# A new order for the first weight loads and adaLN pieces of a conditioned short-convolution layer on one core

## The chip, the core and the metric

The kernel runs on one NeuronCore of a Trainium2 chip. The metric is device time of one execution in microseconds (us); lower is better. TensorE (PE) multiplies and loads weights (PEld), VectorE (DVE) and ScalarE (ACT) do elementwise work, GpSimd (POOL) hardly takes part, and SyncE (SP) issues the loads, one after the other, to 16 DMA engines.

## What is computed

One layer (DEPTH is 1), in float32, for 256 positions, 2048 features and an inner width E of 4096:

```python
h = rmsnorm(x, norm_g)
mod = silu(c) @ ada_w + ada_b            # ada_w: 2048 x 6144
shift, scale, gate = split(mod, 3)
h = h * (1 + scale) + shift
b, c, v, g = split(h @ w_in, 4)          # w_in: 2048 x 16384
u = causal_depthwise_conv(c * v, conv_w) # width 3
y = (b * u * silu(g)) @ w_out            # w_out: 4096 x 2048
out = rmsnorm(x + gate * y, final_g)
```

## The kernel before

Every weight is used once, so the kernel streams 224 MB from HBM. A float32 product is made of three float32r products: ScalarE rounds a loaded tile to `hi` (line 347), VectorE makes `lo`, the rest (line 348), the activations `hT` are split in the same way, and TensorE adds up hi·hi, hi·lo and lo·hi (line 485). So 1 MiB of weights is 48 matmuls, one cast on ScalarE and one subtraction on VectorE.

adaLN must be done before features can be used. `shift` and `scale` are sums over 2048 rows of `ada_w`, weighted by `silu(c)`. The 2048 features are 16 tiles of 128 (numbered from 0) and are made ready two at a time. Tiles 0 and 1 come first, in the opening part of the program (lines 216 to 412). For each later pair VectorE adds up 16 products: 8 **pieces** of 0.5 MiB each, two DMAs and two products to a piece (`ada_piece`, `ada_sums`, lines 434 to 457; the first product of a pair is line 455, the others 457). After the eighth, TensorE transposes the sums, ScalarE adds them up, and `modulate` (line 322) makes the two tiles of `hT`: the high part on ScalarE (339), the rest on VectorE (340 and 341). I number the pieces of tiles 2 and 3 from 0 to 7; 8 and on belong to tiles 4 and 5.

While few tiles are ready, the kernel works on many outputs at once. `plan` (line 56) lists steps: which chunks of 512 outputs of which quarter of `w_in`, with which feature tiles. `parts` (line 523) runs a step in **loads** (`raw_s`) of 1 MiB. I number them: load 1, of 0.5 MiB, is the second step's; loads 2 to 8 take feature tiles 0 and 1 for two chunks each; load 9, used by **block 9** of products, is the first that takes tiles 2 and 3; load 10 and on go back to the first chunks with them. A load's products go to one or two PSUM banks (`mm_s`, three buffers), which ScalarE copies to `acc` (line 517) or VectorE adds (519) before the bank is used again; in a later step ScalarE may first copy `acc` into the bank (533).

What sets the order: the instructions of each engine, and SP's DMAs, run in the order of the built program, each waiting for its inputs and buffers. Within the program a scheduler chooses the order by its own estimates; the kernel ties it down in places. `PACE` says how many adaLN pieces follow each of the first ten loads (the first entry is the opening block, which needs no load here). `first_loads` counts the DMAs that keep the written order on SP, `first_pieces` the loads whose casts and subtractions, with the adaLN products between them, keep it on ScalarE and VectorE. Pieces have four buffers (`at`), loads three (`raw`).

Later the kernel goes through the other outputs with all features ready (`mm_b`, from about 370 us), with the products for `gate` between (`at_g`, lines 616 to 633, already from about 210 us), and at the end through `w_out` (`mm_o`).

Of the kernel before, what the change touches and what calls it, by code (L numbers as in the profile page):

```python
# [49 lines left out]


SHARE = 1.5
PACE = (0, 0, 0, 2, 1, 2, 2, 2, 2, 2)


def plan():
# [36 lines left out]
    while new or any(k < KT for k in done.values()):  # L93
# [30 lines left out]
        if p in order:  # L124
            done[p] = hi
    blocks = [b for step in steps for b in step[-1]][: len(PACE)]
    some = [piece for b in blocks for piece in b]
    for b, n in zip(blocks, PACE):
        b[:], some = some[:n], some[n:]
# [5 lines left out]
def short_conv_layer(ctx: ExitStack, tc: tile.TileContext, x, c, norm_g, ada_w, ada_b, w_in, conv_w, w_out, final_g, out):  # L135
# [83 lines left out]
    for n in range(KT // 4):  # L219
        at = wpool.tile([P, SLOT], F32, tag=("lo", "hi")[n % 2], name="at0", bufs=3)  # L220
        at = at.rearrange("p (k s f) -> p k s f", k=4, s=2)
        if n == 0:
            wpool.tile([P, 32], F32, tag="line3", name="line3", bufs=1)
        for j, kk in ((0, 2), (2, 2)) if n < 3 else ((0, 1), (1, 1), (2, 1), (3, 1)):
            for s in range(2):
                nc.sync.dma_start(at[:, j : j + kk, s, :], adas[:, 4 * n + j : 4 * n + j + kk, s, 0 : NK0 * P])
        first_ada.extend(at[:, i] for i in range(4))
# [239 lines left out]
        modulate(k0, nk, (gs[:, 0:nk], gs[:, nk : 2 * nk]))  # L467

    opener = [None]
    first_loads = [None] * 28  # L470

    def load(dst, src):

# [44 lines left out]
        else:  # L518
            nc.vector.tensor_tensor(out=acc[ch, q], in0=bank, in1=acc[ch, q], op=ALU.add)

    first_pieces = [None] * 10

    def parts(chs, q, k0, k1, seeds, between):

# [272 lines left out]
```

## Time and profile before

| | |
|---|---|
| time, median of 3 runs | 929.32 us (929.06 to 929.54) |
| the profiled execution | 930.7 us, span 928.6 us |
| TensorE busy | 901.8 us (97%) |
| VectorE busy | 629.7 us (68%) |
| ScalarE busy | 453.4 us (49%) |
| mean granted TensorE clock | 0.993 |
| read from HBM | 224.49 MB |

A row of a timeline has start and duration in us, engine, source line, instruction, what it writes and reads with shapes, how many are merged, and in brackets how long the engine was idle before it and what ended that. A matmul's duration is longer than its share of a stream, because matmuls overlap. The span runs from the first to the last instruction; the time of a run includes what lies around it.

### The profile page before, as it was taken

The numbers are of one execution on the slowest core, as the hardware profiler recorded it, in microseconds if no ns is written. First come the engines' busy times: TensorE is split into PE (matmuls) and PEld (weight loads), VectorE is DVE, ScalarE is ACT, GpSimd is POOL, SyncE is SP. The second block draws the span as 40 slices with busy tenths as digits, with TensorE's granted clock in tenths as the row PEclk, the third lists the DMA queues.
The fourth block names the chain that finished last, engine by engine and source line by source line (L and its number), as shares of the span: only waits on it lengthen the run. The fifth ranks groups of instructions, "written<-read, shape, count | busy, mean of one in ns | idle before, by whom it ended". The sixth has DMA issues, their size and how long they took to land.

```text
span 928.6 us, 16211 instructions
## 1 busy us (share of the span) xinstructions
PE 901.8 (97%) x7041; PEld 862.6 (93%) x7041; DVE 629.7 (68%) x603; ACT 453.4 (49%) x431; POOL 2.3 (0%) x9
## 2 busy tenths in 40 slices
PE   7988999999999999999999999999999999999996
PEld 4887999999999989999999999999999988888885
DVE  5678998999897899885455545544554544545882
ACT  6656885565544765643443344334433433344333
POOL 1000000000000000000000000000000000000000
PEclk9998999999999999999999999999999999999999
DMA  9899999999897769667666566656665496556542
GB/s 295 312 315 382 341 360 356 336 341 340 316 342 266 254 245 325 203 214 222 188 200 202 181 192 204 196 183 197 204 188 183 139 359 227 181 191 207 192 136 91
DMA packets 146807, 227.64 MB, mean 245 GB/s; under 512 B 5488, under 2 KB 103840, under 8 KB 146352
## 3 DMA queue, kind: packets, MB, share of 16 engines
q1 hardware_dynamic: 146608, 226.51, 72.6%
q8 instruction: 55, 0.90, 0.4%
q14 instruction: 16, 0.13, 0.0%
q0 software_dynamic: 96, 0.08, 0.0%
q10 hardware_dynamic: 32, 0.01, 0.0%
HBM read 224.49 MB, written 2.10 MB: 244 GB/s over the span
## 4 chain that ended last, share of the span: by engine, by line
PE 83%; DMA 8%; DVE 5%; issue 2%; ACT 2%; SPq 1%; ACTq 0%; DVEq 0%
PE mm_b L485 37%; PE mm_s L485 26%; PE mm_o L693 6%; PE mm_o L694 6%; PE mm_o L695 6%; DMA at<-in_ada_w_dram 3%; DMA raw_s<-in_sc_w_in_dram 3%; DMA at_g<-in_ada_w_dram 2%; DVE lo L348 2%; ACT hi L347 1%; DVE gacc L625 1%; DVE gv L457 1%; DVE acc L419 0%; DVE acc L422 0%; PE tp_g L464 0%
## 5 line engine op out<-in xcount | busy, mean ns | idle before, releaser
L485 PE MATMUL mm_s<-hT,hi 128*128 128x256 f32 x2048 | 342.1, 279 | 13.1 <-ACT acc L517 4.2
L485 PE MATMUL mm_b<-hT,hi 128*128 128x256 f32 x2048 | 348.4, 276 | 0.0
L485 PEld LDWEIGHTS mm_s<-hT,hi 128*128 128x128 f32 x2048 | 303.0, 190 | 15.8 <-ACT acc L517 4.8
L485 PEld LDWEIGHTS mm_b<-hT,hi 128*128 128x128 f32 x2048 | 308.2, 188 | 0.0
L485 PE MATMUL mm_b<-hT,lo 128*128 128x256 f32 x1024 | 282.6, 276 | 0.0
L485 PE MATMUL mm_s<-hT,lo 128*128 128x256 f32 x1024 | 263.4, 277 | 0.0
L348 DVE TENSOR_TENSOR lo<-raw,hi 128x2048 fp32r<-128x2048 f32 x64 | 146.7, 2292 | 133.6 <-ACT hi L347 133.6
L347 ACT CAST hi<-raw 128x2048 fp32r<-128x2048 f32 x64 | 122.4, 1913 | 199.9 <-PE mm_b L485 152.4
L485 PEld LDWEIGHTS mm_b<-hT,lo 128*128 128x128 f32 x1024 | 192.2, 188 | 0.1
L485 PEld LDWEIGHTS mm_s<-hT,lo 128*128 128x128 f32 x1024 | 184.1, 189 | 0.0
L347 ACT CAST hi<-raw_s 128x2048 fp32r<-128x2048 f32 (+1 forms) x64 | 121.5, 1899 | 109.8 <-PE mm_s L485 84.4
L348 DVE TENSOR_TENSOR lo<-raw_s,hi 128x2048 fp32r<-128x2048 f32 (+1 forms) x64 | 145.4, 2272 | 28.9 <-ACT hi L347 26.4
L348 DVE TENSOR_TENSOR lo<-raw_o,hi 128x2048 fp32r<-128x2048 f32 x32 | 73.3, 2291 | 64.3 <-ACT hi L347 64.3
L347 ACT CAST hi<-raw_o 128x2048 fp32r<-128x2048 f32 x32 | 61.0, 1907 | 106.8 <-PE mm_o L695 85.3
L694 PE MATMUL mm_o<-lo,y 128*128 128x512 f32 x256 | 99.3, 389 | 0.0
L695 PE MATMUL mm_o<-hi,y 128*128 128x512 f32 x256 | 99.3, 389 | 0.0
L693 PE MATMUL mm_o<-hi,y 128*128 128x512 f32 x256 | 99.3, 389 | 0.0
L457 DVE SCALAR_TENSOR_TENSOR gv<-at,silu_c,gv 128x512 f32<-128x512 f32 x105 | 78.5, 749 | 2.3 <-DMA at<-in_ada_w_dram 0.6
L695 PEld LDWEIGHTS mm_o<-hi,y 128*128 128x128 f32 x256 | 48.1, 188 | 10.0
L693 PEld LDWEIGHTS mm_o<-hi,y 128*128 128x128 f32 x256 | 48.1, 188 | 9.9
L694 PEld LDWEIGHTS mm_o<-lo,y 128*128 128x128 f32 x256 | 48.1, 188 | 9.9
L517 ACT COPY acc<-mm_s 128x1024 f32<-128x1024 f32 x43 | 42.9, 1013 | 16.8 <-PE mm_s L485 16.8
(109 smaller groups left out, 376.5 us busy)
## 6 DMA issues: line engine op xcount, KB each, us to landing
raw<-in_sc_w_in_dram SPq DMA_DIRECT2D x64, 1024.0 KB, 5.6
raw_s<-in_sc_w_in_dram SPq DMA_DIRECT2D x63, 1024.0 KB, 7.1
raw_o<-in_sc_w_out_dram SPq DMA_DIRECT2D x32, 1024.0 KB, 5.2
at<-in_ada_w_dram SPq DMA_DIRECT2D x124, 256.0 KB, 7.2
at_g<-in_ada_w_dram SPq DMA_DIRECT2D x32, 512.0 KB, 6.7
x<-in_x_dram SPq DMA_DIRECT2D x4, 512.0 KB, 6.5
big<-in_x_dram SPq DMA_DIRECT2D x2, 1024.0 KB, 7.3
out_dram<-big SPq DMA_DIRECT2D x4, 512.0 KB, 2.9
```

The source lines that it names most:

```text
L347: nc.scalar.copy(hi[:, :n], raw[:, :n])
L348: nc.vector.tensor_tensor(out=lo[:, :n], in0=raw[:, :n], in1=hi[:, :n].bitcast(F32), op=ALU.subtract)
L457: nc.vector.scalar_tensor_tensor(out=gv, in0=at4[:, i], scalar=c_k, in1=gv, op0=ALU.mult, op1=ALU.add)
L485: mm = last_mm[0] = nc.tensor.matmul(dst, w, h[:, k], start=begins and left, stop=ends, skip_group_check=True)
L517: nc.scalar.copy(acc[ch, q], bank)
L625: nc.vector.scalar_tensor_tensor(out=ga, in0=at3[:, i, :], scalar=s, in1=ga, op0=ALU.mult, op1=ALU.add)
L693: nc.tensor.matmul(po, yh, hi[:, o], start=opens, stop=False, skip_group_check=True)
L694: nc.tensor.matmul(po, yh, lo[:, o], start=False, stop=False, skip_group_check=True)
L695: nc.tensor.matmul(po, yl, hi[:, o], start=False, stop=ct == NCT - 1, skip_group_check=True)
```

## The change

Four numbers change, and no arithmetic.

```diff
-PACE = (0, 0, 0, 2, 1, 2, 2, 2, 2, 2)
+PACE = (0, 0, 2, 1, 2, 1, 2, 1, 2, 2)
...
-        for j, kk in ((0, 2), (2, 2)) if n < 3 else ((0, 1), (1, 1), (2, 1), (3, 1)):
+        for j, kk in ((0, 2), (2, 2)) if n < 3 else ((0, 2), (2, 1), (3, 1)):
...
-    first_loads = [None] * 28
+    first_loads = [None] * 10
...
-    first_pieces = [None] * 10
+    first_pieces = [None] * 4
```

The pieces that follow the first ten loads are 13 as before, but begin one load sooner and are spread more evenly. Of the opening's adaLN rows for tiles 0 and 1 (`at0`), the last four k rows come as one pair and two single ones, not as four single ones. The order is written out for the first 10 DMAs and for four loads' parts; beyond that the scheduler chooses.

SP, from load 2 on (`raw_s` is a load, `at` a piece, two DMAs each). Before:

```order
L474 DMA raw_s<-in_sc_w_in_dram 128x2x1024 x2
L474 DMA at<-in_ada_w_dram 128x2x256 x4
L474 DMA raw_s<-in_sc_w_in_dram 128x2x1024
L474 DMA at<-in_ada_w_dram 128x2x256 x2
L474 DMA raw_s<-in_sc_w_in_dram 128x2x1024
L474 DMA at<-in_ada_w_dram 128x2x256 x4
L474 DMA raw_s<-in_sc_w_in_dram 128x2x1024
L474 DMA at<-in_ada_w_dram 128x2x256 x4
L474 DMA raw_s<-in_sc_w_in_dram 128x2x1024
L474 DMA at<-in_ada_w_dram 128x2x256 x4
```

and now:

```order
L474 DMA raw_s<-in_sc_w_in_dram 128x2x1024
L474 DMA at<-in_ada_w_dram 128x2x256 x4
L474 DMA raw_s<-in_sc_w_in_dram 128x2x1024
L474 DMA at<-in_ada_w_dram 128x2x256 x4
L474 DMA raw_s<-in_sc_w_in_dram 128x2x1024 x2
L474 DMA at<-in_ada_w_dram 128x2x256 x2
L474 DMA raw_s<-in_sc_w_in_dram 128x2x1024 x2
L474 DMA at<-in_ada_w_dram 128x2x256 x2
L474 DMA raw_s<-in_sc_w_in_dram 128x2x1024
L474 DMA at<-in_ada_w_dram 128x2x256 x2
L474 DMA raw_s<-in_sc_w_in_dram 128x2x1024
L474 DMA at<-in_ada_w_dram 128x2x256 x4
```

Pieces 0 and 1 moved ahead of load 3, pieces 2 and 3 ahead of load 4, piece 4 behind load 5; piece 7 (the first two DMAs of the last row of both) moved from behind load 7 to behind load 9.

VectorE, from load 2's low part on in both (128x2048 is a load's low part, `gv` an adaLN product of tiles 2 and 3). Before:

```order
L348 TENSOR_TENSOR lo<-raw_s,hi 128x2048 x2
L455 TENSOR_SCALAR gv<-at,silu_c 128x512
L348 TENSOR_TENSOR lo<-raw_s,hi 128x2048
L457 SCALAR_TENSOR_TENSOR gv<-at,silu_c,gv 128x512 x3
L348 TENSOR_TENSOR lo<-raw_s,hi 128x2048
L457 SCALAR_TENSOR_TENSOR gv<-at,silu_c,gv 128x512 x5
```

and now:

```order
L348 TENSOR_TENSOR lo<-raw_s,hi 128x2048
L455 TENSOR_SCALAR gv<-at,silu_c 128x512
L457 SCALAR_TENSOR_TENSOR gv<-at,silu_c,gv 128x512
L348 TENSOR_TENSOR lo<-raw_s,hi 128x2048
L457 SCALAR_TENSOR_TENSOR gv<-at,silu_c,gv 128x512
L348 TENSOR_TENSOR lo<-raw_s,hi 128x2048
L457 SCALAR_TENSOR_TENSOR gv<-at,silu_c,gv 128x512
L348 TENSOR_TENSOR lo<-raw_s,hi 128x2048
L457 SCALAR_TENSOR_TENSOR gv<-at,silu_c,gv 128x512 x3
L348 TENSOR_TENSOR lo<-raw_s,hi 128x2048
L457 SCALAR_TENSOR_TENSOR gv<-at,silu_c,gv 128x512 x4
```

Both products of piece 0 now stand ahead of load 3's low part, where before the second stood behind load 4's. From load 4's low part to the low part of `hT` for tiles 2 and 3 (line 341) there stand seven low parts of loads in both programs, with 23 products of line 457 before and 20 now.

ScalarE, from load 4's cast (`hi`) on; the copies are those of the banks of loads 2, 3 and (the last row of the second fence) of the second bank of load 3. Before:

```order
L347 CAST hi<-raw_s 128x2048
L517 COPY acc_401<-mm_s 128x1024
L517 COPY acc_403<-mm_s 128x1024
L347 CAST hi<-raw_s 128x2048
L517 COPY acc_472<-mm_s 128x1024
L517 COPY acc_474<-mm_s 128x1024
L347 CAST hi<-raw_s 128x2048
```

and now:

```order
L347 CAST hi<-raw_s 128x2048
L517 COPY acc_410<-mm_s 128x1024
L347 CAST hi<-raw_s 128x2048
L517 COPY acc_412<-mm_s 128x1024
L517 COPY acc_475<-mm_s 128x1024
L347 CAST hi<-raw_s 128x2048
L517 COPY acc_477<-mm_s 128x1024
```

The second copy of each load moved behind the cast of one more load: that of load 2's second bank from ahead of load 5's cast to behind it.

## The prediction

> **What bounds the kernel now.** I read the page first, then TensorE's timeline for its idle times, then the timelines of the engines named there, each for the same stretch.
>
> ```profile
> span 928.6 us, 16211 instructions
> PE 901.8 (97%) x7041; PEld 862.6 (93%) x7041; DVE 629.7 (68%) x603; ACT 453.4 (49%) x431; POOL 2.3 (0%) x9
> PEclk9998999999999999999999999999999999999999
> ```
>
> TensorE is busy for 97% of the span, so little can be won except where it waits, and the clock row shows one dip, in the fourth slice of 23.2 us. These are its waits once the products have begun (start, duration, instruction, idle time before it and what ended that):
>
> ```profile
> 28.83 2.55 PE L485 MATMUL mm_s<-hT,hi 128*128 128x256 f32 x20 [0.72 <-ACT hi L347]
> 42.05 2.10 PE L485 MATMUL mm_s<-hT,hi 128*128 128x256 f32 x16 [1.22 <-ACT acc L517]
> 56.19 2.10 PE L485 MATMUL mm_s<-hT,hi 128*128 128x256 f32 x16 [2.98 <-ACT acc L517]
> 77.83 0.62 PE L485 MATMUL mm_s<-hT,hi 128*128 128x256 f32 x3 [1.48 <-ACT hT L339]
> 81.29 4.00 PE L485 MATMUL mm_s<-hT,hi 128*128 128x256 f32 x17 [2.84 <-DVE hT L341]
> 104.80 0.50 PE L485 MATMUL mm_s<-hT,hi 128*128 128x256 f32 x2 [1.52 <-ACT mm_s L533]
> 330.99 0.51 PE L485 MATMUL mm_s<-hT,hi 128*128 128x256 f32 x2 [2.19 <-DVE acc L519]
> ```
>
> The two largest together, 1.48 + 2.84 = 4.32 us, come before block 9, the first that needs feature tiles 2 and 3: TensorE ran out of work at 76.35 (77.83 - 1.48) and the tiles were whole only at 81.3. They cost more than their length, as the clock says (columns after the times: busy us and count of PE, PEld, DVE, ACT, POOL, then clock, DMA share, GB/s):
>
> ```profile
> 40.00:45.00 5.00, 3.78 (x33) 3.58 (x32) 3.81 (x4) 4.70 (x4) 0.00 (x0) 1.00 0.52 183
> 45.00:50.00 5.00, 5.00 (x47) 5.00 (x46) 4.93 (x5) 1.95 (x3) 0.00 (x0) 1.00 0.90 247
> 55.00:60.00 5.00, 3.81 (x33) 3.81 (x34) 4.64 (x5) 3.05 (x4) 0.00 (x0) 1.00 0.79 286
> 70.00:75.00 5.00, 5.00 (x46) 5.00 (x46) 5.00 (x9) 4.36 (x12) 0.00 (x0) 1.00 1.05 380
> 75.00:80.00 5.00, 1.97 (x15) 1.57 (x14) 4.41 (x6) 3.27 (x4) 0.00 (x0) 0.90 1.04 393
> 80.00:85.00 5.00, 3.71 (x17) 3.71 (x18) 4.74 (x7) 1.91 (x1) 0.00 (x0) 0.50 1.08 377
> 85.00:90.00 5.00, 5.00 (x42) 5.00 (x41) 2.76 (x4) 2.15 (x2) 0.00 (x0) 0.91 1.06 371
> ```
>
> Work done at a lower clock: 0.10 x 1.97 + 0.50 x 3.71 + 0.09 x 5.00 = 2.5 us lost. So **block 9's late features cost 4.3 + 2.5 = 6.8 us**. Why they are late stands on VectorE, which makes the last part of them (L341):
>
> ```profile
> 41.12 2.29 DVE L348 TENSOR_TENSOR lo<-raw_s,hi 128x2048 fp32r<-128x2048 f32 x1 [2.84 <-ACT hi L347]
> 43.33 2.32 DVE L457 SCALAR_TENSOR_TENSOR gv<-at,silu_c,gv 128x512 f32<-128x512 f32 x3
> 45.57 2.28 DVE L348 TENSOR_TENSOR lo<-raw_s,hi 128x2048 fp32r<-128x2048 f32 x1
> 55.26 2.29 DVE L348 TENSOR_TENSOR lo<-raw_s,hi 128x2048 fp32r<-128x2048 f32 x1 [3.59 <-ACT hi L347]
> 67.98 2.29 DVE L348 TENSOR_TENSOR lo<-raw_s,hi 128x2048 fp32r<-128x2048 f32 x1 [2.03 <-ACT hi L347]
> 80.82 0.75 DVE L341 TENSOR_TENSOR hT<-xs,hT 128x256 fp32r<-128x256 f32 x2
> L457 DVE SCALAR_TENSOR_TENSOR gv<-at,silu_c,gv 128x512 f32<-128x512 f32 x105 | 78.5, 749 | 2.3 <-DMA at<-in_ada_w_dram 0.6
> ```
>
> From load 4's low part (41.12) to the features' end (81.57) are 40.45 us, of which VectorE waited 3.59 + 2.03 = 5.62, both times for ScalarE's cast of a load: 34.8 us are work. The loads were late because SP stood still:
>
> ```profile
> 35.09 9.90 SPq L474 DMA_DIRECT2D at<-in_ada_w_dram  x4
> 45.09 0.41 SPq L474 DMA_DIRECT2D raw_s<-in_sc_w_in_dram  x1
> 51.06 9.31 SPq L474 DMA_DIRECT2D at<-in_ada_w_dram  x4
> 60.46 0.93 SPq L474 DMA_DIRECT2D raw_s<-in_sc_w_in_dram  x2
> ```
>
> For 9.90 us it held the issue of pieces 3 and 4, then for 9.31 us that of pieces 7 and 8, since a piece needs one of four buffers. Piece 4 needs piece 0's, and piece 0's second product stands on VectorE behind load 4's low part, at 43.33. Behind piece 4 stood load 6 (45.09). The DMA engines fell to 183 and 247 GB/s against 380 when fed.
>
> **The change part by part.** It adds and removes no arithmetic. The loads of the first features in fewer pieces save two issues on SP; load 1 is then issued some 0.7 us sooner. That is worth between 0.7 us (the whole wait at 28.83) and nothing, if the DMA engines are the limit there; a loss would need a product to wait for the pair that now lands together, and another two k rows follow it anyway. I take 0.
>
> The rest is one thing, a new order, and I walk it with the durations above. ScalarE's casts give the rate of the stream (each of these casts waited for its own DMA):
>
> ```profile
> 30.41 1.91 ACT L347 CAST hi<-raw_s 128x2048 fp32r<-128x2048 f32 x1 [1.63 <-DMA raw_s<-in_sc_w_in_dram]
> 33.65 1.92 ACT L347 CAST hi<-raw_s 128x2048 fp32r<-128x2048 f32 x1 [0.42 <-DMA raw_s<-in_sc_w_in_dram]
> 39.18 1.91 ACT L347 CAST hi<-raw_s 128x2048 fp32r<-128x2048 f32 x1 [2.71 <-DMA raw_s<-in_sc_w_in_dram]
> 40.99 1.92 ACT L517 COPY acc<-mm_s 128x1024 f32<-128x1024 f32 x2
> 43.21 1.92 ACT L347 CAST hi<-raw_s 128x2048 fp32r<-128x2048 f32 x1 [0.30 <-DMA raw_s<-in_sc_w_in_dram]
> 53.33 1.90 ACT L347 CAST hi<-raw_s 128x2048 fp32r<-128x2048 f32 x1 [6.38 <-DMA raw_s<-in_sc_w_in_dram]
> ```
>
> Loads 2 to 5 came at 30.41, 33.65, 39.18 and 43.21: 12.8 us for 4.5 MiB (a load is 1 MiB, a piece 0.5), 2.84 us per MiB; the steps by themselves give 2.69 to 3.24. In the new order pieces 0 and 1 go ahead of load 3 and pieces 2 and 3 ahead of load 4, so load 3 lands at 30.4 + 2 x 2.84 = 36.1 (2.4 later than now) and load 4 at 41.8 (2.6 later). Then load 5 at 44.6, load 6, behind piece 4, at 48.9 (53.3 now), load 7 at 51.7, load 8 at 56.0, load 9 at 60.2, load 10 at 65.9. No issue holds SP long: both products of piece 0 now stand ahead of load 3's low part, so piece 4's buffer is free by 40.
>
> TensorE pays at first. Load 3's bank waits for the copy of load 1's, which stands behind load 3's cast: 36.1 + 1.8 + 1.0 = 38.9, a wait of 1.0 (TensorE is free at 37.9). Its second bank waits for the copy behind load 4's cast, 41.8 + 1.8 + 1.0 = 44.6, against 41.6: 3.0. Load 4's first bank waits for a copy that now stands behind load 5's cast (ScalarE goes on 44.6 + 1.8 + 1.0 = 47.4, TensorE is free at 47.3): 0.1. After that each copy is done before it is asked for. With the 0.72 at 28.83 that is 4.8, against 0.72 + 1.22 + 2.98 = 4.92 now: TensorE reaches block 9 at 76.2.
>
> VectorE: load 4's low part starts at 41.8 + 1.9 = 43.7. From there to the features the order holds the same seven low parts and 20 adaLN products instead of 23: 34.8 - 3 x 0.75 = 32.6 us, and none of it waits: by the same walk the casts of loads 5 to 10 are over 0.3 to 4 us before VectorE reaches them. The features are whole at 43.7 + 32.6 = 76.3, 5.3 us sooner than now. Block 9's wait falls to 0.1 and the clock has no reason to drop.
>
> Sum: 6.8 (block 9) + 0.1 (waits ahead of it) - 0.1 (what is left) = **6.8 us less** by 105 us. What is late next is the 1.52 us at 104.80 (ScalarE's order, unmoved). Later on only 330.99 shows a wait, so the gain stays. The profiled execution took 930.7 around its span of 928.6, 1.4 above the median of 929.32; taken off the median the time is **922.5 us**.
>
> Bounds: at 3.24 us per MiB load 4 comes at 43.4 and the features at 77.9, 1.6 us worse; at 2.69, 0.6 better for VectorE, but TensorE is then the later one. The wait at 330.99 is hidden or not by VectorE's order among the gate's products, which is new too: between 2.2 us less and (rival 3) all of the gain. I take it as unchanged, since the copy that ends it has the same neighbours.
>
> **The rivals.** 1. The clock drops at the new wait of 3.0 us. At 56.19 a wait of 2.98 left the clock at 1.00, and one pair of 4.32 took it to 0.50, so the point lies between. A drop would cost what it cost in 80 to 85, some 1.9 us: 924.4. The Trainium skill ("TensorE: Matmul & The Clock Gate", Part 1, The HAM clock gate) puts it at an idle window of about 3.4 us that runs freely; both waits of this trace agree, and by that rule this rival needs load 4 to come 0.4 us later than I have it.
>
> 2. One of loads 4 to 6 comes some 2.5 us late, as load 6 did for lack of a full queue. These three have least to spare (0 to 0.5 us), so the features are 2.5 late: 925.0; with the clock dropping again, 927. For it: load 7's issue must wait for load 4's buffer (its low part ends at 45.9), when only load 6 is under way. Against: two loads and a piece are queued ahead until then.
>
> 3. The gain is given back at 330.99. The chain runs from 268 to 331 over VectorE and the gate's DMAs alone:
>
> ```profile
> 246.21 21.83 PE mm_s L485 x192
> 273.67 7.15 DMA at_g<-in_ada_w_dram
> 330.99 67.24 PE mm_s L485 x576
> ```
>
> If it went by its own pace, an earlier TensorE would only wait longer: 929.3. Against it: at its upper end it hangs on TensorE, and 2.19 us in 63 is a small lag.
>
> 4. **Slower.** Piece 7, the last that features 2 and 3 need, is moved on SP from behind load 7 to behind load 9: 11 MiB after load 2 instead of 9, or 2 x 2.84 = 5.7 us later. If SP stands still as it does now, the features come at 81.6 + 5.7 = 87.3 and the time is 935. By the stream piece 7 lands at 30.4 + 11 x 2.84 = 61.6, and VectorE asks for it at about 64; slower than before it is only if SP loses a further 2.4 + 5.3 = 7.7 us, most of a 9.90. VectorE's order around it has room, and piece buffers are freed a load earlier, which speaks against.
>
> **How the numbers follow.** No change is anything within 0.2% (1.9 us, about what a measurement of this kernel can tell). My forecast has 0.49; with the wait at 330.99 gone as well (920.3) 0.06; rival 1 0.13; rival 2 0.14: faster 0.82. Rival 3 or a mixture that nets nothing 0.10. Rival 4 0.08. The range from 919.8 to 928.0 leaves out rival 4 and most of rival 3.
>
> **What would show it.** Right: SP issues loads 4 to 9 with no piece holding it near 10 us; DMA at 350 GB/s or more from 40 to 60; a TensorE wait of about 1 us near 39 and 3 near 44; none over 1 us between 50 and 90, with the clock at 1.00 in 80 to 85; features 2 and 3 whole near 76. Wrong: VectorE waiting for a cast after 46; waits at block 9; a wait near 320 to 335 of more than 3 us, which would mean that the gain was lent, not won.

## The result and the profile after

| kernel | median us | runs | ratio to before (95% interval) |
|---|---|---|---|
| before | 929.19 | 6, 927.70 to 931.46 | 1 |
| changed | 921.45 | 6, 919.56 to 922.25 | 0.9914 (0.9898 to 0.9929) |

The change is worth 7.7 us of 929. The profiled execution of the changed kernel took 920.8 us around a span of 919.0.

The page of the changed kernel: the span, the busy times, and the granted clock in slices of 23 us, which has lost the dip in its fourth slice.

```profile
span 919.0 us, 16211 instructions
PE 898.6 (98%) x7041; PEld 859.8 (94%) x7041; DVE 629.6 (69%) x603; ACT 453.9 (49%) x431; POOL 2.3 (0%) x9
PEclk9999999999999999999999999999999999999999
```

TensorE's timeline of the changed kernel, its waits since the products began (last column: idle time before, and what ended it):

```profile
37.23 2.15 PE L485 MATMUL mm_s<-hT,hi 128*128 128x256 f32 x16 [0.68 <-ACT acc L517]
42.78 3.48 PE L485 MATMUL mm_s<-hT,hi 128*128 128x256 f32 x16 [2.46 <-ACT acc L517]
96.52 0.51 PE L485 MATMUL mm_s<-hT,hi 128*128 128x256 f32 x2 [1.53 <-ACT mm_s L533]
322.91 0.50 PE L485 MATMUL mm_s<-hT,hi 128*128 128x256 f32 x2 [2.40 <-DVE acc L519]
```

No row stands between 43 and 96: block 9 waits for nothing. The two waits at 104.80 and 330.99 are there as before, 8.3 and 8.1 us sooner. Two waits for the copy of a bank are new in place: the prediction had them near 39 and near 44, and they end at 37.23 and 42.78. The second has a drop of the clock behind it. The windows of the changed kernel show that drop, and that there is none in 75 to 85 (columns as in the prediction: clock, DMA share and GB/s last):

```profile
40.00:45.00 5.00, 2.54 (x13) 2.33 (x12) 3.15 (x3) 5.00 (x4) 0.00 (x0) 0.73 0.91 335
45.00:50.00 5.00, 5.00 (x43) 5.00 (x41) 4.93 (x5) 4.21 (x5) 0.00 (x0) 0.93 0.96 321
50.00:55.00 5.00, 5.00 (x47) 5.00 (x46) 4.89 (x6) 3.81 (x3) 0.00 (x0) 1.00 1.03 374
55.00:60.00 5.00, 5.00 (x47) 5.00 (x46) 4.67 (x5) 3.79 (x3) 0.00 (x0) 1.00 1.05 375
75.00:80.00 5.00, 5.00 (x45) 4.85 (x44) 4.93 (x7) 1.35 (x2) 0.00 (x0) 1.00 1.05 377
80.00:85.00 5.00, 4.92 (x44) 4.72 (x43) 4.63 (x5) 5.00 (x5) 0.00 (x0) 1.00 1.04 380
```

The drop cost 0.27 x 2.54 + 0.07 x 5.00 = 1.0 us. Of the 350 GB/s or more that the prediction asked for from 40 to 60 us, the first two windows stay below (335 and 321); the mean of the four is 351.

VectorE's timeline of the changed kernel, from load 4's low part to the features:

```profile
41.85 2.29 DVE L348 TENSOR_TENSOR lo<-raw_s,hi 128x2048 fp32r<-128x2048 f32 x1 [2.59 <-ACT hi L347]
59.17 2.29 DVE L348 TENSOR_TENSOR lo<-raw_s,hi 128x2048 fp32r<-128x2048 f32 x1 [0.26 <-ACT hi L347]
64.61 2.29 DVE L348 TENSOR_TENSOR lo<-raw_s,hi 128x2048 fp32r<-128x2048 f32 x1 [0.76 <-ACT hi L347]
74.72 0.75 DVE L341 TENSOR_TENSOR hT<-xs,hT 128x256 fp32r<-128x256 f32 x2
```

The waits of 3.59 and 2.03 us for casts have become 0.26 and 0.76, and the features are whole at 75.5 instead of 81.6. From load 4's low part to there VectorE waits 1.6 us in all where it waited 6.2, and works 32.1 us where it worked 34.2. The rows of SP's queue are the reason for the shorter waits; its longest rows from 24 to 56 us are now four piece DMAs in 4.68 us and two loads in 5.91 (which wait for a buffer of the loads):

```profile
24.27 4.68 SPq L474 DMA_DIRECT2D at<-in_ada_w_dram  x4
38.63 5.91 SPq L474 DMA_DIRECT2D raw_s<-in_sc_w_in_dram  x2
```

### The profile page after: what moved, and what is told of

Same layout as the page of the kernel before. It is cut to its first block, busy times and chain, and to the rows that moved or that the text cites. A ratio compares the mean times of both kernels' runs of the same rounds, so it can differ in the third digit from the quotient of the medians.

```text
span 919.0 us, 16211 instructions
## 1 busy us (share of the span) xinstructions
PE 898.6 (98%) x7041; PEld 859.8 (94%) x7041; DVE 629.6 (69%) x603; ACT 453.9 (49%) x431; POOL 2.3 (0%) x9
## 4 chain that ended last, share of the span: by engine, by line
PE 91%; DMA 4%; DVE 2%; ACT 1%; issue 1%; SPq 0%; ACTq 0%
PE mm_b L485 38%; PE mm_s L485 34%; PE mm_o L693 6%; PE mm_o L695 6%; PE mm_o L694 6%; DMA at<-in_ada_w_dram 2%; DMA raw_s<-in_sc_w_in_dram 1%; DVE lo L348 1%; ACT hi L347 1%; DMA x<-in_x_dram 1%; DVE acc L419 0%; PE tp_g L464 0%; DVE acc L422 0%; DVE gacc L625 0%; DVE acc L570 0%
## 5 line engine op out<-in xcount | busy, mean ns | idle before, releaser
L517 ACT COPY acc<-mm_s 128x1024 f32<-128x1024 f32 x43 | 43.3, 1011 | 18.9 <-PE mm_s L485 18.9
```

The source lines that it names most:

```text
L517: nc.scalar.copy(acc[ch, q], bank)
```

## The experiments

Ratios are to the kernel before, run on the same chip each time ("small" and "2+1+1" are the two ways to load the first features, the numbers after them the DMAs and parts in fixed order):

| kernel | PACE | first features | fixed order | median us | ratio (95% interval) |
|---|---|---|---|---|---|
| before | old | small | 28, 10 | 927.9, 929.5, 927.4 | 1 |
| e1 | new | small | 28, 10 | 918.58 | 0.9903 (0.9882 to 0.9923) |
| e2 | old | 2+1+1 | 28, 10 | 926.97 | 0.9988 (0.9974 to 1.0001) |
| e3 | old | small | 10, 4 | 917.13 | 0.9887 (0.9868 to 0.9906) |
| e4 | old, one product moved | small | 28, 10 | 920.40 | 0.9918 (0.9900 to 0.9937) |
| e5 | new | small | 10, 4 | 921.85 | 0.9932 (0.9912 to 0.9951) |
| e6 | new | 2+1+1 | 28, 10 | 917.47 | 0.9870 (0.9853 to 0.9888) |
| e7 | old | 2+1+1 | 10, 4 | 914.73 | 0.9847 (0.9828 to 0.9866) |
| changed | new | 2+1+1 | 10, 4 | 921.45 | 0.9914 (0.9898 to 0.9929) |
| e8 | new | 2+1+1 | 14, 4 | 912.99 | 0.9827 (0.9809 to 0.9844) |

And what one profiled execution of each shows, in us. "SP held" is SP's idle time before the issue of a piece, between 22 and 70 us, counting only standstills of 1.8 us and more; waits for the buffer of a load are not in it. "features" is when features 2 and 3 are whole; then come TensorE's waits by place (25 to 70 us; block 9; up to 110 us for a bank that line 533 fills; later), and the busy time lost to a lower clock in windows of 5 us.

| kernel | SP held | features | 25-70 | block 9 | L533 | later | clock | span | span less these |
|---|---|---|---|---|---|---|---|---|---|
| before | 18.9 | 81.6 | 4.9 | 4.3 | 1.5 | 2.2 | 3.9 | 928.6 | 911.8 |
| e1 | 13.3 | 79.3 | 5.5 | 0 | 0 | 0 | 1.5 | 918.1 | 911.1 |
| e2 | 19.4 | 81.9 | 3.7 | 4.4 | 1.5 | 0 | 4.0 | 924.6 | 911.0 |
| e3 | 1.9 | 74.5 | 1.4 | 0 | 1.8 | 0.5 | 0 | 915.5 | 911.8 |
| e4 | 12.7 | 76.6 | 2.6 | 1.1 | 1.1 | 0 | 0 | 916.9 | 912.1 |
| e5 | 1.9 | 78.3 | 5.4 | 0 | 1.5 | 0 | 1.6 | 919.1 | 910.6 |
| e6 | 11.1 | 75.9 | 4.6 | 0 | 0 | 0 | 0 | 914.4 | 909.8 |
| e7 | 0 | 71.8 | 0.6 | 0 | 1.8 | 2.9 | 1.7 | 917.4 | 910.4 |
| changed | 2.2 | 75.5 | 3.1 | 0 | 1.5 | 2.4 | 1.0 | 919.0 | 911.0 |
| e8 | 0 | 69.7 | 1.5 | 0 | 0 | 0 | 0 | 911.3 | 909.8 |

The last column stays within 909.8 and 912.1 us while the spans differ by 17: nearly all the time by which these kernels differ stands in the five columns from "25-70" to "clock". (e7's profile is the slowest of its five executions, 919.2.)

**e1, the new PACE alone.**

```
-PACE = (0, 0, 0, 2, 1, 2, 2, 2, 2, 2)
+PACE = (0, 0, 2, 1, 2, 1, 2, 1, 2, 2)
```

> The kernel before with the new PACE alone (first features still in small pieces, 28 DMAs and ten parts in fixed order). Theory A, the prediction's: the gain comes from pieces 0 to 3 standing ahead of loads 3 and 4, which frees piece 4's buffer before SP asks for it. Then no piece holds SP for near 10 us before load 8, features 2 and 3 are whole by 78 us, block 9 waits under 1 us, and most of the gain of the whole change is here: 921 to 925 us. Rival B: the shorter fixed order (10 DMAs) is what lets loads pass pieces on SP; then SP still stands still for 5 us or more between 35 and 60, the features come after 79, and the time is 926 us or more.

918.58 us, below A's range, and yet not by A's way. SP's queue shows that it stood still from 38.08 to 45.59 for the next piece, with load 6 behind it:

```profile
37.67 0.41 SPq L474 DMA_DIRECT2D raw_s<-in_sc_w_in_dram  x1
45.59 0.88 SPq L474 DMA_DIRECT2D at<-in_ada_w_dram  x2
46.56 0.42 SPq L474 DMA_DIRECT2D raw_s<-in_sc_w_in_dram  x1
```

Load 6 landed at 54.89, later than before (53.25), VectorE waited 3.75 us for it, and the features were whole at 79.3: B's first two signs, without B's time. What PACE alone did: VectorE had less to do up to the features (from load 4's low part 31.0 us instead of 34.2, with six low parts of loads instead of seven), so that they came 2.3 us sooner, and tile by tile (the first at 78.3); TensorE came to block 9 later (a drop of the clock at 58 us cost it 1.5), and met no wait there. The wait for a copy of line 533 is gone as well. Both theories fail in part.

**e2, the loads of the first features alone.**

```
-((0, 1), (1, 1), (2, 1), (3, 1))
+((0, 2), (2, 1), (3, 1))
```

> The kernel before with only the loads of the first features changed (the last group in 2 + 1 + 1 k rows instead of 1 + 1 + 1 + 1). All other instructions keep their order. Theory A, the prediction's term of 0 (at most the wait of 0.72 at 28.83): the time is 928.5 to 929.3. Theory C, from the two traces (load 1 landed at 25.2 instead of 27.7, load 2 at 27.8 instead of 30.3): the issues saved let the DMA queue run full from 20 to 28 us, everything after load 1 comes about 2 us sooner, the wait at 28.83 goes and block 9's features come 1.5 to 2 us sooner, so that the time falls by 1.3 to 2.5 us, to 926.7 to 927.9.

926.97 against 927.86, 0.9 us less, between the two theories, and its interval reaches just over 1. The loads came sooner, as theory C said: load 1 landed at 25.49 instead of 27.71, load 6 at 51.98 instead of 53.25. But SP then stood still for pieces as long as ever (19.4 us), VectorE waited 3.69 us for load 8, and features 2 and 3 came at 81.9, no sooner:

```profile
33.16 10.34 SPq L474 DMA_DIRECT2D at<-in_ada_w_dram  x4
49.55 8.31 SPq L474 DMA_DIRECT2D at<-in_ada_w_dram  x4
```

**e3, the shorter fixed order alone.**

```
-first_loads = [None] * 28
+first_loads = [None] * 10
-first_pieces = [None] * 10
+first_pieces = [None] * 4
```

> The kernel before with only the fixed order shortened (10 DMAs on SP, 4 parts). On SP three loads now stand behind pieces 2 and 3, and pieces 4 to 6 behind load 7, so that no load stands behind a piece that waits for a buffer. Theory A (SP standing still for a piece's buffer makes load 6 late): load 6 lands by 49 instead of 53.3, VectorE's wait of 3.59 at 55.26 is under 1 us, but the pieces come later, so the features come at 77 to 81 and the time is 923 to 927. Rival B (the shorter fixed order changes nothing by itself, the pieces' own arrival sets the features): 928 to 930.

917.13 us, better than either theory and at least as good as the whole change. On SP loads 5 to 7 now follow pieces 2 and 3, and pieces hold SP for 1.9 us instead of 18.9. SP's queue (the middle row waits for buffers of the loads), then VectorE's last step of the features:

```profile
29.72 3.99 SPq L474 DMA_DIRECT2D at<-in_ada_w_dram  x4
34.38 8.44 SPq L474 DMA_DIRECT2D raw_s<-in_sc_w_in_dram  x3
43.11 4.03 SPq L474 DMA_DIRECT2D at<-in_ada_w_dram  x6
```

```profile
74.03 0.42 DVE L341 TENSOR_TENSOR hT<-xs,hT 128x256 fp32r<-128x256 f32 x1
```

Load 6 landed at 46.98 instead of 53.25, VectorE waits at most 0.64 us between 47 and 81, the features are whole at 74.5, and block 9 waits for nothing. Theory A had the mechanism, but expected the pieces to come late; only piece 4 did (landed at 51.16 instead of 48.09), and piece 7, the last that the features need, came at 58.11 instead of 60.35.

**e4, one product moved.** Nothing of the change is in this kernel; one adaLN product of 0.75 us goes ahead of load 4's low part on VectorE.

```
-with behind(ended if first_pieces or j + i == 0 else {}):
+with behind(ended if first_pieces or j + i == 0 else {}, advance=j + i == 1 and len(first_pieces) > 5):
```

> The kernel before with one adaLN product moved on VectorE: the second of piece 0 now stands ahead of load 4's low part instead of behind it; the DMAs up to load 7 keep their order on SP. Theory A (piece 4's buffer comes free only behind load 4's low part, and that is what holds SP from 35.5 to 44.1, behind which load 6 stands): SP's 9.90 us at 35.09 fall to under 4, load 6 is issued before 41 instead of 45.09 and its cast begins 3 to 5 us before 53.33, VectorE's wait of 3.59 us falls to under 1, features 2 and 3 come 2 to 5 us before 81.57, and the time is 923 to 927. Rival D (load 6 is late for the buffer of an earlier load, or because its own transfer is slow; the piece only shares the wait): its cast stays within 1 us of 53.3 and the time within 0.2% of before.

920.40 us, 7.5 less. SP's queue, ScalarE's cast of load 6, and the features' end:

```profile
34.84 4.37 SPq L474 DMA_DIRECT2D at<-in_ada_w_dram  x4
39.31 0.41 SPq L474 DMA_DIRECT2D raw_s<-in_sc_w_in_dram  x1
```

```profile
48.15 1.91 ACT L347 CAST hi<-raw_s 128x2048 fp32r<-128x2048 f32 x1 [2.10 <-DMA raw_s<-in_sc_w_in_dram]
```

```profile
59.07 2.29 DVE L348 TENSOR_TENSOR lo<-raw_s,hi 128x2048 fp32r<-128x2048 f32 x1 [3.48 <-ACT hi L347]
75.88 0.76 DVE L341 TENSOR_TENSOR hT<-xs,hT 128x256 fp32r<-128x256 f32 x2
```

The row of 9.90 us is one of 4.37 (theory A said under 4), load 6 is issued at 39.31 instead of 45.09, its cast begins 5.2 us sooner, the features are whole 4.9 us sooner (76.6). VectorE's long wait did not vanish: it moved to load 7 (3.48 us at 59.07), behind the next pieces (4.95 us on SP at 43.97). Rival D is out. This is the closest test of the mechanism: up to load 7 one product of 0.75 us is all that stands elsewhere, and load 6 is issued 5.8 and cast 5.2 us sooner. What comes after is less pure, since from load 8 on the scheduler's order differs too: of the 4.9 us of the features 2.0 are shorter waits of VectorE, 2.0 are three adaLN products fewer between load 4's low part and them (the moved one among the three), and 0.9 a load 4 that came sooner by itself. Block 9's wait falls from 4.3 to 1.1 us with no drop of the clock.

**e5, the changed kernel with the first features in small pieces.**

```
-((0, 2), (2, 1), (3, 1))
+((0, 1), (1, 1), (2, 1), (3, 1))
```

> The changed kernel with the loads of the first features put back into small pieces (1 + 1 + 1 + 1 k rows); order of everything else as in the changed kernel, whose ratio to before is 0.9914. Theory A, the prediction's term of 0 for this edit: ratio 0.990 to 0.9925. Theory C (the full DMA queue from 20 to 28 us brings loads 1 to 10 about 2 us sooner, and in the changed kernel TensorE waits for just these): load 3 lands at 36 and load 4 at 41.8 as the prediction had it, the wait near 44 is 3 us or more instead of 2.46, and the ratio is 0.993 to 0.996.

921.85 us, 0.9932, at the lower edge of theory C; the intervals of 0.9932 and 0.9914 overlap. The traces are clear on the mechanism: load 3 lands at 36.88 and load 4 at 42.43 (34.29 and 39.84 in the changed kernel), and both waits for banks are longer, 2.36 instead of 0.68 and 2.53 instead of 2.46:

```profile
39.83 2.11 PE L485 MATMUL mm_s<-hT,hi 128*128 128x256 f32 x16 [2.36 <-ACT acc L517]
45.37 3.54 PE L485 MATMUL mm_s<-hT,hi 128*128 128x256 f32 x16 [2.53 <-ACT acc L517]
```

Over the four pairs in the table that differ in this edit alone it is worth 0.0012 (before and e2), 0.0018 (e5 and changed), 0.0033 (e1 and e6) and 0.0040 (e3 and e7) of the time: 1 to 4 us, always the same way, though only in the last pair do the intervals lie apart.

**e6, the changed kernel with the long fixed order.**

```
-first_loads = [None] * 10
+first_loads = [None] * 28
-first_pieces = [None] * 4
+first_pieces = [None] * 10
```

> The changed kernel with the long fixed order put back (28 DMAs, ten parts). Three loads then go between pieces 2 to 4 on SP, and on ScalarE the copies of the banks of load 3 stand ahead of load 5's cast. Theory E (PACE alone gave 0.9903 and the shorter order alone 0.9887, the change 0.9914: either frees SP, and together they put load 4 behind two more pieces, which is the wait of 2.46 at 42.78): without the shorter order that wait is under 1.6 us and the ratio is 0.987 to 0.990. Rival F (the shorter order adds to the gain of PACE, or at least costs nothing): ratio 0.9914 or more.

917.47 us, 0.9870: theory E. The wait after load 4's copy is 1.08 at 41.77. Another of 2.71 stands at 55.68, without a drop of the clock, for load 6, which SP held back for 8.6 us as in e1. Rival F is out: with the new PACE the shorter order costs 3 to 4 us (0.9870 against 0.9914, intervals apart; against 0.9905 in the repeat r1 they still overlap), though it takes SP's hold away.

**e7, the changed kernel with the old PACE.**

```
-PACE = (0, 0, 2, 1, 2, 1, 2, 1, 2, 2)
+PACE = (0, 0, 0, 2, 1, 2, 2, 2, 2, 2)
```

> The changed kernel with the old PACE: the two other edits together. Theory E (the shorter order by itself frees SP, the new PACE costs the waits at 37.23 and 42.78): ratio 0.986 to 0.989, no wait over 1.6 us between 30 and 90. Rival A (the prediction's: PACE is what brings the features forward, and the rest counts for nothing): ratio 0.9914 or more.

914.73 us, 0.9847: better still than theory E's range. No wait reaches 1 us between 30 and 90, and no piece holds SP. Without the new PACE the other two edits gain nearly twice what the change gains; with it they lose 6 us of that.

**e8, 14 DMAs in fixed order.**

```
-first_loads = [None] * 10
+first_loads = [None] * 14
```

> The changed kernel with 14 instead of 10 DMAs in fixed order. SP then issues load 4 behind piece 2 and ahead of piece 3, so it lands about 1.5 us sooner. Theory E: the wait of 2.46 at 42.78 falls to 1 to 1.5, with it the clock has no drop there, features still before TensorE is free, ratio 0.986 to 0.989, the best of all so far. Rival G (the wait at 42.78 is made up elsewhere: at 96.52 and 322.91, where VectorE and ScalarE set the pace): those two waits grow by what this one loses, and the ratio stays within 0.0015 of 0.9914.

912.99 us, 0.9827, the fastest of all; its interval lies apart from the changed kernel's. TensorE's group of products on its page, beside the same row of the kernel before and of the changed one (busy us, mean ns, then the idle time and what ended most of it):

```profile
L485 PE MATMUL mm_s<-hT,hi 128*128 128x256 f32 x2048 | 336.8, 277 | 1.5 <-ACT acc L517 1.5
```

```profile
L485 PE MATMUL mm_s<-hT,hi 128*128 128x256 f32 x2048 | 342.1, 279 | 13.1 <-ACT acc L517 4.2
```

```profile
L485 PE MATMUL mm_s<-hT,hi 128*128 128x256 f32 x2048 | 338.9, 278 | 7.1 <-ACT acc L517 3.1
```

The wait after load 4 is 1.06, since load 4 now goes ahead of piece 3 and lands at 38.72 instead of 39.84. Rival G, that this would be made up at 96.52 and 322.91, is out: those waits are gone too. That is more than theory E said. The first goes with TensorE's order: in e1, e6 and e8 all products of block 9's two banks stand ahead of the next bank's, while in the other kernels of the table the next bank's first products, which need a copy of line 533, stand between them; all of those show this wait (1.06 to 1.53 us in one place, or 1.8 in two), and none of these three. The second comes and goes by itself (below).

**r1, r2 and r3, the changed kernel twice more and the kernel before once more.** No edit.

> The changed kernel itself, once more, for its clock. Theory H (whether a TensorE wait of 2 to 3 us costs a clock drop is decided by when it falls, not by its length; so far waits of 2.19 to 2.8 us had a drop in six cases and of 2.37 to 2.98 us none in four): the same two waits, near 42.8 and near 322.9, drop or not differently from the first profile in at least one of the repeats, at lengths within 0.3 us of it, and each drop costs 1.2 to 1.7 us. Rival I (the length and the matmuls around it decide): both repeats show the first profile's picture, a drop at the first wait and none at the second. Ratio 0.990 to 0.993.

> The changed kernel a third time, profile only, with the same expectations of the two theories as for the repeat before it.

> The kernel before once more, profile only. Theory H: the waits near 56.2 (2.98 us, no drop in the first profile) and near 331 (2.19 us, drop) may show it the other way round; the pair before block 9 (4.3 us within 7 us) drops again. Rival I: no drop at 56, a drop at 331. Both: SP stands still for 9 to 10 us near 35 and near 51, features 2 and 3 whole at 81 to 82.

r1 gave 0.9905 (0.9873 to 0.9938), the first result again. The same wait of the changed kernel, in the first profile 2.46 us with a drop, was 2.56 with a drop in r1 (1.4 us lost) and 2.55 without any in r2. r2's wait and the window behind it:

```profile
42.81 2.08 PE L485 MATMUL mm_s<-hT,hi 128*128 128x256 f32 x16 [2.55 <-ACT acc L517]
```

```profile
45.00:50.00 5.00, 5.00 (x45) 5.00 (x44) 4.93 (x5) 4.95 (x5) 0.00 (x0) 1.00 0.97 325
```

And the wait of the kernel before at 56.19, 2.98 us at full clock in the first profile, had in r3 2.60 us and a drop:

```profile
56.61 3.10 PE L485 MATMUL mm_s<-hT,hi 128*128 128x256 f32 x16 [2.60 <-ACT acc L517]
```

```profile
55.00:60.00 5.00, 3.39 (x19) 3.39 (x20) 4.25 (x4) 3.30 (x4) 0.00 (x0) 0.74 0.78 285
```

Theory H holds, rival I is out. Over all profiles single waits of 2.19 to 2.98 us had a drop in 8 of 14 cases: 2.19, 2.46, 2.53, 2.56, 2.57, 2.60, 2.72 and 2.79 with it, 2.36, 2.40, 2.52, 2.55, 2.71 and 2.98 without. A drop cost 1.0 to 1.7 us.

What parts the two is where the wait falls on a grid of time. The clock records of the traces show that each drop behind a single wait is half clock for 3.41 us (6.83 behind the pair at block 9), and in every trace with more than one stretch of half clock after 25 us these begin a whole number of 3.41 us apart (where a trace has only the half clock after its last product, the grid is counted back from there). The next windows are laid on that grid, the wait of 2.56 us in r1 first, then that of 2.55 us in r2 (the second number in each row is TensorE's busy time):

```profile
40.25:43.66 3.41, 1.15 (x10) 1.15 (x11) 2.08 (x1) 3.41 (x3) 0.00 (x0) 1.00 1.06 383
43.66:47.07 3.41, 3.41 (x19) 3.41 (x18) 3.41 (x4) 3.07 (x4) 0.00 (x0) 0.50 0.79 253
```

```profile
38.45:41.86 3.41, 1.81 (x16) 1.61 (x15) 0.83 (x2) 1.91 (x2) 0.00 (x0) 1.00 1.07 388
41.86:45.28 3.42, 2.47 (x21) 2.47 (x22) 3.40 (x3) 3.42 (x3) 0.00 (x0) 1.00 0.73 271
```

In r1 2.3 us of the wait lie in one cell of the grid, and the clock halves with the next cell; in r2 the wait is split 1.60 to 0.95, and nothing happens. So it is in all 14 cases: with a drop TensorE is idle for 2.00 to 2.79 us of the cell before it, without one for at most 1.93 us of any cell (the wait of 2.98 us in the kernel before is split 1.93 to 1.04). This was found in the traces afterwards and no run was made to test it, and the limit is not sharp: the pair at block 9 in e2 brought a drop after a cell with 1.77 us of idle time.

The wait of the gate stage comes and goes as well: 2.40 us at 322.91, gone in r1, 2.52 in r2; 2.19 in the kernel before and under 0.6 in r3.

**r4, three buffers for pieces instead of four.**

```
-name="at", bufs=4
+name="at", bufs=3
```

(and the same for the gate's two names that share them)

> The changed kernel with three buffers for the pieces instead of four (the gate's tiles share them). Theory A (the gain rests on no piece holding SP for a buffer): SP again stands still for 4 us or more at a piece between 30 and 65, loads behind it come late, features 2 and 3 come at 79 us or later, TensorE waits at block 9 for 2 to 6 us, and most of the gain is gone: ratio 0.996 to 1.003. Rival J (the written order of pieces and loads is what counts, buffers are slack): ratio within 0.002 of 0.9914.

937.23 us, 1.0104 (1.0075 to 1.0134), worse than theory A's range, and rival J is out. Block 9 waits again, 1.59 + 3.63 us, for features whole at 78.8. But up to 70 us no piece holds SP for as much as 1.8 us: with fewer buffers the scheduler placed the pieces later instead, and from 188 to 345 us many small waits follow that no other kernel here has. So this run shows that the buffers count, and does not single out SP's hold; e4 and e3 do.

## Why the prediction came out right, and where it did not

**Block 9, the main term (6.8 us): right.** Of the 4.3 us of waits and 2.5 us of clock nothing is left. The features are whole at 75.5 (I had 76.3), VectorE's waits between are 1.6 us in sum (I had none). Before they were 6.2 and not 5.6: I counted a wait of 0.59 us for a piece, at 75.98, as work. With that put right the work left is 34.2 - 3 x 0.75 = 32.0 us, and 32.1 was measured. TensorE came to block 9 at 74.7 (I had 76.2). That SP was held by pieces whose buffer hangs on one adaLN product is shown by e4, and that this made the features late by e3, where VectorE's waits fall from 6.2 to 1.0 us, and in part by e4; in the changed kernel pieces hold SP for 2.2 us instead of 18.9.

**The walk of the loads: right in shape, 2 us late.** Loads 3 to 9 landed at 34.29, 39.84, 42.41, 46.28, 49.78, 54.24 and 58.23, where I had 36.1, 41.8, 44.6, 48.9, 51.7, 56.0 and 60.2. Without the edit of the first features (e5) load 3 came at 36.88 and load 4 at 42.43, close to my walk. So the step that failed is the term of 0 for that edit. Its bound of 0.7 us counted only TensorE's next wait and the 0.7 us by which the issue comes sooner. In fact load 1 landed 2.5 us sooner (25.20 instead of 27.71). From 20 to 25 us the DMA engines moved 367 GB/s where they had moved 271; the window of the kernel before, then that of the changed one:

```profile
20.00:25.00 5.00, 5.00 (x36) 4.35 (x34) 3.53 (x9) 3.51 (x6) 0.00 (x0) 1.00 0.87 271
```

```profile
20.00:25.00 5.00, 4.88 (x32) 3.99 (x31) 3.35 (x8) 3.28 (x6) 0.00 (x0) 1.00 1.04 367
```

The edit is worth 1 to 4 us in the pairs above.

**The waits that TensorE would pay first: right in place, too large in sum.** I had 0.72 + 1.0 + 3.0 + 0.1 = 4.8 us; it was 0.68 + 2.46 = 3.1.

**The clock (rival 1, given 0.13): it happened, and I had priced it out for a wrong reason.** "The point lies between" 2.98 and 4.32 us was wrong: the length of a wait alone does not decide. The first trace already held the evidence against it, in a row that I had quoted for another purpose: behind the wait of 2.19 us at 330.99 stands this window of the kernel before, which I had not read.

```profile
330.00:335.00 5.00, 4.01 (x21) 4.01 (x22) 5.00 (x6) 2.94 (x3) 0.00 (x0) 0.66 0.58 197
```

There the clock fell and 1.4 us were lost. By r1 to r3 there is no such point between 2.2 and 3.0 us: the 2.98 us at 56.19 left the clock alone, and no cell of the grid held 2.0 us of them. An estimate from that grid: a wait of 3.0 us puts 2.0 us or more into one cell of 3.41 us in (3.41 - 1.0) / 3.41 = 0.7 of all places, so that rival 1 deserved far more than 0.13. The rule of the Trainium skill that I put beside it ("TensorE: Matmul & The Clock Gate", Part 1, The HAM clock gate) speaks of one idle window of about 3.4 us that runs freely. The traces agree with the free running and with the length (the grid of 3.41 us), and differ in the idle time that is enough: single waits of 2.19 to 2.79 us had a drop.

**The later waits: right in the first profile, but not fixed.** 1.53 at 96.52 and 2.40 at 322.91 stand as I said. That the profiled span fell by 9.6 us, and the median by 7.7, may come in part from the drop at 331, which the first profile of before had and that of the changed kernel had not.

**Why the sum came out so near.** Block 9 gave its 6.8 us, the waits ahead of it 1.8 (4.9 to 3.1, where I had 0.1), and the clock took 1.0 back: 7.6 of the 8.3 us by which the wait at 96.52 comes sooner. The term of the first features was too small and the chance of a clock drop too low, and the two errors had opposite signs: that 921.45 lies so near 922.5 is in part luck.

**What the prediction missed altogether: which edit earns the time.** I took the four numbers as one new order, with PACE as its core. Apart, PACE alone (0.9903) and the shorter order alone (0.9887) each bring as much as the whole change (0.9914; the intervals overlap), and together, with the same first features, they bring no more than either: 0.9932 against 0.9903 and 0.9887 with small pieces, and 0.9914 against 0.9870 and 0.9847 with 2+1+1, where the intervals lie apart. SP's hold goes with the shorter order (1.9 us in e3, 0 in e7), not with PACE (13.3 in e1). Where the hold is gone through 10 DMAs in fixed order, PACE only costs: the waits from 25 to 70 us are 1.4 in e3 and 5.4 in e5, 0.6 in e7 and 3.1 in the changed kernel, and in the table each of the two with PACE has a drop of the clock in them. They stand where load 4 goes behind pieces 2 and 3 on SP and a bank's copy behind load 4's cast on ScalarE. With 14 DMAs (e8) load 4 goes ahead of piece 3, the waits are 1.5, and PACE costs nothing that these runs can tell (0.9827 against 0.9847 in e7, overlapping). The step of mine that fails is "TensorE pays at first": it set that cost against the old waits at 42.05 and 56.19, found them even, and did not ask which edit brings which. Rivals 2, 3 and 4 did not come: VectorE waited at most 0.8 us for a load after 46, the wait of the gate stage grew by 0.2 us, and piece 7 landed at 59.8, before VectorE asked for it.

## What to carry to other kernels

When a queue that issues transfers in order stands still, look for the instruction that frees the buffer it waits for, and for what that instruction is queued behind: here one product of 0.75 us in the wrong place held the loads behind it for 8 us. A change of several numbers that gains can hold one that loses: time its parts alone and each left out, since two parts may reach the same wait by different ways and keep both costs. A step taken at nothing because the next wait is small should be followed to the waits behind it: a stream that ran 2 us ahead met them with 2 us to spare.

## What the runs showed of the hardware

- A wait of TensorE between 2.2 and 3.0 us lowered the granted clock in 8 of 14 cases, the same wait of the same kernel in one execution (2.56 us) and not in the next (2.55 us), for 1.0 to 1.7 us each. The drops lie on a grid of 3.41 us that runs through the whole execution, and the 14 cases part by the idle time within one of its cells: 2.00 us and more with a drop, 1.93 and less without. With the wait of the gate stage, which is there in some executions and not in others, this comes together with a spread of 917.3 to 923.1 us in six runs of the changed kernel (r1); e8, with no wait above 1.1 us after 25 us, spread from 912.3 to 913.7 in four.
- A small difference in how the adaLN rows of the opening are issued moved the landing of the next load more than its issue: with the last four rows in single rows load 1 landed between 26.1 and 28.4 us (before, e1, e3, e4, e5), with 2 + 1 + 1 rows between 25.1 and 25.8 (changed, e2, e6, e7, e8), though it was issued at 20.9 to 21.5 in the former and 20.3 to 21.0 in the latter.
